# One decoder layer on one core: block sums of h on VectorE, the last denominators, merged heads in halves, order of loads

## The chip, the cores and the metric

The kernel runs on one core of one Trainium2 chip. The metric is the device time of one execution in microseconds (us); the figure given for a kernel is the median of its runs.

## What is computed

One inference step of a decoder layer for a prompt of 1024 tokens and 8 sample tokens (T = 1032 columns, model width 1024 = 8 blocks of 128). What matters here:

```python
h = rms_norm(x, g_pre)
q, k, v, c_b, c_c, c_h, g_a, g_c = split(h @ w_in)       # 4608 + 5 * 1024 columns
# three head groups with (window, dilation) (128,1), (512,4), (2048,16), 8 heads of 64 each;
# the groups of a head are merged by softmax over their log-denominators
a = merge(attention(q, k, v)) @ w_attn_o                 # 512 -> 1024
c = (c_b * causal_conv3(c_c * c_h)) @ w_conv_o
x = x + rms_norm((sigmoid(g_a) * a + sigmoid(g_c) * c) @ w_o)
x = x + rms_norm(square(relu(rms_norm(x) @ w_ff1)) @ w_ff2)
```

The sample tokens attend to caches of 128, 512 and 1024 rows, and all three caches go out again shifted by one row.

## The kernel before

Every float32 product is split: an operand is a rounded high part and a low part, and a product is three matrix products on TensorE (high by high, high by low, low by high). Weights come from HBM in tiles of 128x512 (SyncE's queue, L169), ScalarE casts the high part (L177) and VectorE or GpSimd subtracts to get the low part (L180). A `plan` lists the weight tiles in the order of their use; `tick`, called after each unit of matmuls, moves tiles through load, sum, cast and subtraction. Tile tracks what each instruction depends on and reorders instructions on each engine; those given to `keep_in_program_order` (`pe`, `pin`) keep the written order among themselves on their engine. A pool that opens where another was closed lies on the same memory, so the first writer of a new tile waits for the last reader of the old ones, a DMA too.

**Attention of the prompt.** A loop over 8 head slots h: scores, maximum, exponentials, products with v. `fill(h)` is a generator that gives the projections of the next head slot in units of 12 matmuls (128x344), run between the steps so that TensorE always has work. For h = 7 there is no next slot: `fill(7)` projects v and then four raw gates (`gate_raw`, L375), 30 units, of which 28 are used up before the loop's end. `den_out(h)` (L745) splits the sums of exponentials (`parts`), yields, reduces them over partitions by four matmuls (L752), copies the row (`den_row`, L753) and stores it in DRAM (`den_d`, L754, on GpSimd's queue); its first half normally runs in the next head slot. `num_d` holds the unnormalised heads in four pairs. `copy_piece(4)` issues four of 57 DMAs that copy caches to their outputs, on ScalarE's queue.

**Block products.** The remaining projections of h by pairs of weight blocks use Strassen's seven products (`strassen`, L1039) instead of eight. They need sums of blocks of h, T1 to T4 (`tsums`, L998): h cut into upper and lower four row blocks (`js`, `ks`) and left and right halves of columns (`t1`, `t2`), 516 columns each. `tsums(0)` and `tsums(2)` each make half of the rows, as operations on 128x1032 elements: T1 and T2 by five subtractions and additions on VectorE, T3 by one, T4 by two on GpSimd; ScalarE casts the high part of T2, T3 and T4 (L1005), VectorE the low part of T2 and T3, GpSimd that of T4 (L1006). They run beside two more raw gates (12 units). At the end T1 is written over the right half of h itself (L1035, L1036). Product p of a Strassen pair reads, in order: T2, h upper left, h upper right (that is T1), T3, h lower left, T4, h lower right. Each product has two parts of 12 matmuls (128x258); one part is called a beat here, 14 beats a pair. The results gather in three accumulators A, B, C of two banks each; after p = 1, 3, 4, 5 and 6 ScalarE and VectorE move them out (L1058 to L1068), and p = 3 goes on in B.

**Drive.** Fourteen pairs run under `drive` (L1099), which also carries out the attention of the sample tokens (`sample_steps`, 72 steps): in two beats of five it takes one step. The first steps transpose q, k and v of the samples (L821, L833), load the denominators, take their reciprocal (L809) and store it (`rden_d`); then come pipelines that load cache rows, multiply on GpSimd and sum on VectorE. The tiles of this stage (E, D1, the tiles of the samples) lie where the sums' pool was.

**Last three pairs and merged heads.** The three pairs left over (`gate_pairs`) run with `split_heads` (L1161) beside them, one step a beat, 37 steps in 42 beats: for each of four pairs of heads, load numerators (512 KB) and reciprocal denominators (2 x 256 KB, broadcast over partitions) on GpSimd's queue, six beats later multiply on VectorE (L1170), then cast and subtract each half (L1175, L1176) into `ah`, `al`. D0 and D1 receive the results and are stored from GpSimd's queue (L1118).

**Projections of attention and convolution.** For i in 8 blocks: `load_gate` (GpSimd's queue, L1207) and `load_cv` (ScalarE's queue, L1212), four buffers each; sigmoid of the gate (L1220), products with `wao`, gating of the result on VectorE (L1224), store of it (L1233), and the split of the convolution's result (L1229, L1230). Then follow the products with w_conv_o and w_o and the two of the MLP.

Of the kernel before, what the change touches and what calls it, by code (L numbers as in the profile page):

```python
# [10 lines left out]
F32 = mybir.dt.float32  # L11
# [7 lines left out]
P = 128  # L19
# [18 lines left out]
def tile_decoder_layer(  # L38
# [253 lines left out]
    def run(g, n=None):  # L292

        while n is None or n > 0:
            if next(g, run) is run:
                return
            n = n and n - 1
# [72 lines left out]
    def copy_piece(n=1):  # L370
        for _ in range(n):
            if pieces:
                tc.keep_in_program_order(nc.scalar.dma_start(*pieces.pop(0)))
# [9 lines left out]
    with ExitStack() as st:  # L383
# [11 lines left out]
        def classes(t):  # L395

            return t.rearrange("p (r j) -> p r j", r=4)
# [374 lines left out]
        for h in range(8):  # L772
            f = fill(h)
            run(dn, 1)
            for j, _ in enumerate(qk_scores()):
                if j in (2, 4, 6, 8):
                    run(f, 1)
                if j == 5:
                    run(dn)
            maximum()  # L780
            run(f, 3)
            max_keys()
            run(f, 2)
            subtract()
            long = h in (2, 4, 6, 7)
            run(f, 5 if long else 3)
            v_place(vts["v01"], 0, 0)
            v_place(vts["v01"], 1, 1)
            if h % 2 == 0:
                v_place_pair(vts["v2"])  # L790
            run(f, 2 if long else 3)
            for j, _ in enumerate(pv_out(h)):
                if long or j % 4 != 1:
                    run(f, 1)
            dn = den_out(h)
            run(f)
            copy_piece(4)
        run(dn)


    def sbank(shape, name):
# [190 lines left out]
    with tc.tile_pool(name="tsum", bufs=1) as ts:  # L992
        T1 = ts.tile([P, 4, HT], F32, name="T1")

        def f32(x):
            return x.bitcast(F32)

        def tsums(j):  # L998
            js, ks = slice(j, j + 2), slice(4 + j, 6 + j)

            def new(name, bufs=1):
                return ts.tile([P, 2, HT], F32, name=name, bufs=bufs)

            def parts(eng, n, t):
                nc.scalar.copy(TS[n][0][:, js], t)  # L1005
                eng.tensor_tensor(TS[n][1][:, js], t, f32(TS[n][0][:, js]), op=OP.subtract)  # L1006
            V, G, S = nc.vector.tensor_tensor, nc.gpsimd.tensor_tensor, OP.subtract
            b12, b22, T2 = new("b12", 2), new("b22", 2), new("T2", 2)
            V(b12, f32(hh[:, js, t2]), f32(hl[:, js, t2]), op=OP.add)
            V(b22, f32(hh[:, ks, t2]), f32(hl[:, ks, t2]), op=OP.add)  # L1010
            V(T1[:, js], b12, f32(hh[:, js, t1]), op=S)
            V(T1[:, js], T1[:, js], f32(hl[:, js, t1]), op=S)
            V(T2, b22, T1[:, js], op=S)
            yield
            parts(nc.vector, 2, T2)
            yield
            yield
            T3, T4 = new("T3"), new("T4")
            V(T3, b22, b12, op=S)
            parts(nc.vector, 3, T3)  # L1020
            G(T4, f32(hh[:, ks, t1]), T2, op=S)
            G(T4, T4, f32(hl[:, ks, t1]), op=OP.add)
            parts(nc.gpsimd, 4, T4)
            yield

        def plain():
            for i in (8, 9):
                yield from gate_raw(i, ts.tile([P, T], F32, name="gr", bufs=2))
        g = plain()
        for _ in zip(tsums(0), tsums(2)):  # L1030
            run(g, 2)
        run(g)
        for j in (0, 2):
            js = slice(j, j + 2)
            nc.scalar.copy(hh[:, js, t2], T1[:, js])  # L1035
            nc.vector.tensor_tensor(hl[:, js, t2], T1[:, js], f32(hh[:, js, t2]), op=OP.subtract)  # L1036
# [38 lines left out]
    with ExitStack() as st:  # L1075
# [23 lines left out]
        def drive(g):  # L1099
            for _ in g:  # L1100
                beat[0] += 1
                store(3)
                if beat[0] % 5 in (1, 3) or short[0]:
                    short[0] = next(steps, None)


# [49 lines left out]
    with tc.tile_pool(name="apool", bufs=1) as apool:  # L1156
# [3 lines left out]
        with tc.tile_pool(name="pre", bufs=1) as pre:  # L1160
            def split_heads():  # L1161
                for n in range(4):
                    ar, rd = (pre.tile([P, NQ], F32, name=nm) for nm in ("num", "rden"))
                    nc.gpsimd.dma_start(ar, num_d[:, n, :])
                    for a in range(2):
                        nc.gpsimd.dma_start(rd[64 * a:64 * a + 64, :],
                                            rden_d[2 * n + a:2 * n + a + 1, :].to_broadcast([64, NQ]))
                    for _ in range(6):
                        yield
                    nc.vector.tensor_tensor(ar, ar, rd, op=OP.mult)  # L1170
                    yield
                    for c in range(2):
                        src = ar.rearrange("p (r j) -> p j r", r=4)[:, P * c:P * c + P]
                        hi, lo = (t[:, n, 512 * c:512 * c + 512].rearrange("p (j r) -> p j r", r=4) for t in (ah, al))
                        nc.scalar.copy(hi, src)  # L1175
                        nc.vector.tensor_tensor(lo, src, hi.bitcast(F32), op=OP.subtract)  # L1176
                        yield
                nc.scalar.copy(ah[:, :, NQ:], asm)
                nc.vector.tensor_tensor(al[:, :, NQ:], asm, ah[:, :, NQ:].bitcast(F32), op=OP.subtract)
                yield  # L1180
            heads = split_heads()
            for pair in gate_pairs:
                D = [pre.tile([P, T], F32, name=f"D{a}") for a in range(2)]
                if pair is gate_pairs[-1]:
                    raw_spaces.pop()
                    nc.gpsimd.dma_start(gr0, g_d[8])
                for _ in strassen(pair, D, stores(D, [g_d[m - 60] for m in pair], None, False)):
                    run(heads, 1)
            run(heads)
            nc.scalar.activation(gr0, gr0, AF.Sigmoid)  # L1190
# [6 lines left out]
        with tc.tile_pool(name="cpool", bufs=1) as cpool:  # L1197
# [3 lines left out]
            with tc.tile_pool(name="sga", bufs=1) as sga:  # L1201
                cvs, grs = [], [gr0]

                def load_gate():
                    if len(grs) < KT:
                        grs.append(sga.tile([P, T], F32, name="gr", bufs=4))
                        nc.gpsimd.dma_start(grs[-1], g_d[7 + len(grs)])  # L1207

                def load_cv():
                    if len(cvs) < KT:  # L1210
                        cvs.append(sga.tile([P, T], F32, name="cv", bufs=4))
                        nc.scalar.dma_start(cvs[-1], cv_d[len(cvs) - 1])  # L1212
                for _ in range(2):
                    load_gate()
                    load_cv()
                for i in range(KT):
                    load_gate()
                    load_cv()
# [363 lines left out]
```

## Time and profile before

| what | value |
| --- | --- |
| median of 3 runs (lowest, highest) | 2033.48 us (2033.07, 2035.68) |
| the profiled execution: its time, its span | 2032.52 us, 2030.7 us |
| mean granted clock of TensorE | 0.983 of full speed |
| TensorE (PE) busy | 1955.0 us, 96% |
| VectorE (DVE) busy | 1243.6 us, 61% |
| ScalarE (ACT) busy | 735.3 us, 36% |
| GpSimd (POOL) busy | 602.6 us, 30% |

The span runs from the first to the last instruction; the execution's own time is 1.8 us more. TensorE is busy nearly all the time, so what is worth looking at is where it is not, and what ended each of its waits. In a row of the timeline, the bracket at the end names how long the engine was idle before it and what released it; where several things were waited for, the row names one.

### The profile page before, as it was taken

What the parts mean: (1) busy time and instruction counts of PE and PEld (TensorE: products, weight loads), DVE (VectorE), ACT (ScalarE), POOL (GpSimd) and SP (SyncE); (2) the same over time, 40 slices, a digit from 0 to 9 for tenths busy, and PEclk for the clock granted to TensorE, in tenths of its full rate; (3) what the DMA queues carried; (4) which work ended last, traced back from release to release, by engine and by line L of the source; (5) the groups of instructions that cost most, each with busy time, mean ns of one, the idle gap of its engine ahead of it and who ended that gap; (6) DMA issues with size and microseconds to landing.
All of it is one profiled execution on the core that took longest, in us unless ns stands there. A gap on an engine that the chain in (4) does not pass through costs nothing. (4 is left out here: it accounts for less than half of the span.)

```text
span 2030.7 us, 33252 instructions
## 1 busy us (share of the span) xinstructions
PE 1955.0 (96%) x13253; PEld 1932.2 (95%) x13253; DVE 1243.6 (61%) x2086; ACT 735.3 (36%) x1448; POOL 602.6 (30%) x487
## 2 busy tenths in 40 slices
PE   7999999999998899999999999999999999999996
PEld 6999999999998799999999999999999999999995
DVE  7688768777756787897554423735544444454545
ACT  4355435544442333333343333452222222222242
POOL 3233313332334674662412222211111111111113
PEclk8999999999999899999999999999999999999998
DMA  4221343144334363331665431322222322222102
GB/s 146 59 87 38 108 131 128 59 129 131 111 101 164 113 205 109 126 116 54 186 251 165 138 102 46 94 91 86 84 94 84 125 94 84 94 94 83 53 22 84
DMA packets 85995, 216.74 MB, mean 107 GB/s; under 512 B 12000, under 2 KB 22368, under 8 KB 84944
## 3 DMA queue, kind: packets, MB, share of 16 engines
q1 hardware_dynamic: 68736, 119.12, 18.2%
q10 hardware_dynamic: 8112, 68.78, 10.0%
q0 software_dynamic: 8992, 26.72, 4.4%
q8 instruction: 104, 1.70, 0.3%
q14 instruction: 51, 0.42, 0.1%
HBM read 184.17 MB, written 84.86 MB: 132 GB/s over the span
## 5 line engine op out<-in xcount | busy, mean ns | idle before, releaser
L180 POOL TENSOR_TENSOR wl<-wr,wh 128x512 fp32r<-128x512 f32 x152 | 201.9, 1329 | 804.4 <-ACT wh L177 707.6
L177 ACT CAST wh<-wr 128x512 fp32r<-128x512 f32 x320 | 195.3, 619 | 526.5 <-PE ps_mm L260 272.4
L257 PE MATMUL ps_mm<-hh,wh 128*128 128x344 f32 x1008 | 329.7, 327 | 2.5 <-ACT hh L346 1.9
L260 PE MATMUL ps_mm<-hl,wh 128*128 128x344 f32 x1008 | 324.2, 322 | 3.7 <-DVE hl L340 1.9
L261 PE MATMUL ps_mm<-hh,wl 128*128 128x344 f32 x1008 | 323.4, 321 | 0.0
L261 PE MATMUL ps_mm<-rh,wl 128*128 128x344 f32 x768 | 246.4, 321 | 0.0
L257 PE MATMUL ps_mm<-rh,wh 128*128 128x344 f32 x768 | 246.4, 321 | 0.0
L260 PE MATMUL ps_mm<-rl,wh 128*128 128x344 f32 x768 | 245.7, 320 | 0.0
L260 PE MATMUL ps_mm<-gl,wh 128*128 128x344 f32 x768 | 244.9, 319 | 0.8 <-DVE gl L1303 0.8
L257 PE MATMUL ps_mm<-gh,wh 128*128 128x344 f32 x768 | 245.5, 320 | 0.0
L261 PE MATMUL ps_mm<-gh,wl 128*128 128x344 f32 x768 | 244.7, 319 | 0.0
L1419 DVE TENSOR_TENSOR f<-ps_mm,f 128x344 f32<-128x344 f32 x336 | 170.4, 515 | 111.5 <-PE ps_mm L261 110.9
L180 DVE TENSOR_TENSOR wl<-wr,wh 128x512 fp32r<-128x512 f32 x168 | 139.7, 832 | 152.8 <-ACT wh L177 152.4
L260 PEld LDWEIGHTS ps_mm<-hl,wh 128*128 128x128 f32 x1008 | 190.8, 189 | 5.7 <-DVE hl L340 3.2
L257 PEld LDWEIGHTS ps_mm<-hh,wh 128*128 128x128 f32 x1008 | 191.2, 190 | 3.9 <-ACT hh L346 2.9
L261 PEld LDWEIGHTS ps_mm<-hh,wl 128*128 128x128 f32 x1008 | 190.7, 189 | 0.0
L260 PEld LDWEIGHTS ps_mm<-gl,wh 128*128 128x128 f32 x768 | 144.2, 188 | 1.2 <-DVE gl L1303 1.1
L260 PEld LDWEIGHTS ps_mm<-rl,wh 128*128 128x128 f32 x768 | 144.8, 189 | 0.0
L261 PEld LDWEIGHTS ps_mm<-rh,wl 128*128 128x128 f32 x768 | 144.8, 189 | 0.0
L257 PEld LDWEIGHTS ps_mm<-rh,wh 128*128 128x128 f32 x768 | 144.8, 189 | 0.0
L257 PEld LDWEIGHTS ps_mm<-gh,wh 128*128 128x128 f32 x768 | 144.3, 188 | 0.0
L261 PEld LDWEIGHTS ps_mm<-gh,wl 128*128 128x128 f32 x768 | 144.1, 188 | 0.0
(326 smaller groups left out, 4555.0 us busy)
## 6 DMA issues: line engine op xcount, KB each, us to landing
wr<-in_win_dram SPq DMA_DIRECT2D x152, 256.0 KB
wr<-in_wf_dram SPq DMA_DIRECT2D x128, 256.0 KB
out_okv_dram<-in_cache_dram ACTq DMA_DIRECT2D x16, 1020.0 KB
kt<-in_cache_dram SPq DMA_DIRECT2D x32, 256.0 KB
x_sb<-in_xT_dram SPq DMA_DIRECT2D x12, 344.0 KB
cv_d<-D SPq DMA_DIRECT2D x16, 258.0 KB
gr<-g_d POOLq DMA_DIRECT2D x8, 516.0 KB, 7.4
cv<-cv_d ACTq DMA_DIRECT2D x8, 516.0 KB
```

The source lines that it names most:

```text
L177: pin_(nc.scalar.copy(hi, raw))
L180: pin_(eng.tensor_tensor(lo, raw, hi.bitcast(F32), op=OP.subtract))
L257: ins = nc.tensor.matmul(ps, wh, rh, start=(first and i == 0), stop=False)
L260: nc.tensor.matmul(ps, wh, rl, start=False, stop=False)
L261: nc.tensor.matmul(ps, wl, rh, start=False, stop=(last and i == n - 1))
L1419: pin(nc.vector.tensor_tensor(d, ps, d, op=OP.add))
```

## The change

The change has five parts. (1) In the last head slot the two units of projection left over are no longer run before the denominators: the split of the sums of exponentials comes first, then one unit, then the reduction, its copy and its store, then the last unit; and four cache copies are no longer issued there (all 57 are still made, in the MLP). (2) T4 and its low part move from GpSimd to VectorE. (3) The sample's steps begin after the first pair of the drive (beat 16 instead of 1). (4) The merged heads go in halves of 512 columns: eight loads of 256 KB and twice eight of 128 KB, four beats between load and use, then multiply and split at once; 41 steps in 42 beats. D0 of the last pairs gets a second buffer. (5) One convolution result fewer is loaded ahead of the loop over i.

```diff
--- before.py
+++ after.py
@@ -793,9 +793,13 @@
                 if long or j % 4 != 1:
                     run(f, 1)
             dn = den_out(h)
-            run(f)
-            copy_piece(4)
+            if h < 7:
+                run(f)
+                copy_piece(4)
+        run(dn, 1)
+        run(f, 1)
         run(dn)
+        run(f)
 
 
     def sbank(shape, name):
@@ -1001,10 +1005,10 @@
             def new(name, bufs=1):
                 return ts.tile([P, 2, HT], F32, name=name, bufs=bufs)
 
-            def parts(eng, n, t):
+            def parts(n, t):
                 nc.scalar.copy(TS[n][0][:, js], t)
-                eng.tensor_tensor(TS[n][1][:, js], t, f32(TS[n][0][:, js]), op=OP.subtract)
-            V, G, S = nc.vector.tensor_tensor, nc.gpsimd.tensor_tensor, OP.subtract
+                nc.vector.tensor_tensor(TS[n][1][:, js], t, f32(TS[n][0][:, js]), op=OP.subtract)
+            V, S = nc.vector.tensor_tensor, OP.subtract
             b12, b22, T2 = new("b12", 2), new("b22", 2), new("T2", 2)
             V(b12, f32(hh[:, js, t2]), f32(hl[:, js, t2]), op=OP.add)
             V(b22, f32(hh[:, ks, t2]), f32(hl[:, ks, t2]), op=OP.add)
@@ -1012,15 +1016,15 @@
             V(T1[:, js], T1[:, js], f32(hl[:, js, t1]), op=S)
             V(T2, b22, T1[:, js], op=S)
             yield
-            parts(nc.vector, 2, T2)
+            parts(2, T2)
             yield
             yield
             T3, T4 = new("T3"), new("T4")
             V(T3, b22, b12, op=S)
-            parts(nc.vector, 3, T3)
-            G(T4, f32(hh[:, ks, t1]), T2, op=S)
-            G(T4, T4, f32(hl[:, ks, t1]), op=OP.add)
-            parts(nc.gpsimd, 4, T4)
+            parts(3, T3)
+            V(T4, f32(hh[:, ks, t1]), T2, op=S)
+            V(T4, T4, f32(hl[:, ks, t1]), op=OP.add)
+            parts(4, T4)
             yield
 
         def plain():
@@ -1100,7 +1104,7 @@
             for _ in g:
                 beat[0] += 1
                 store(3)
-                if beat[0] % 5 in (1, 3) or short[0]:
+                if beat[0] > 14 and beat[0] % 5 in (1, 3) or short[0]:
                     short[0] = next(steps, None)
 
 
@@ -1160,17 +1164,17 @@
         with tc.tile_pool(name="pre", bufs=1) as pre:
             def split_heads():
                 for n in range(4):
-                    ar, rd = (pre.tile([P, NQ], F32, name=nm) for nm in ("num", "rden"))
-                    nc.gpsimd.dma_start(ar, num_d[:, n, :])
-                    for a in range(2):
-                        nc.gpsimd.dma_start(rd[64 * a:64 * a + 64, :],
-                                            rden_d[2 * n + a:2 * n + a + 1, :].to_broadcast([64, NQ]))
-                    for _ in range(6):
-                        yield
-                    nc.vector.tensor_tensor(ar, ar, rd, op=OP.mult)
-                    yield
                     for c in range(2):
-                        src = ar.rearrange("p (r j) -> p j r", r=4)[:, P * c:P * c + P]
+                        ar, rd = (pre.tile([P, 512], F32, name=nm) for nm in ("num", "rden"))
+                        js = slice(P * c, P * c + P)
+                        nc.gpsimd.dma_start(classes(ar), classes(num_d[:, n, :])[:, :, js])
+                        for a in range(2):
+                            nc.gpsimd.dma_start(classes(rd[64 * a:64 * a + 64, :]),
+                                                classes(rden_d[2 * n + a:2 * n + a + 1, :])[:, :, js].to_broadcast([64, 4, P]))
+                        for _ in range(4):
+                            yield
+                        nc.vector.tensor_tensor(ar, ar, rd, op=OP.mult)
+                        src = ar.rearrange("p (r j) -> p j r", r=4)
                         hi, lo = (t[:, n, 512 * c:512 * c + 512].rearrange("p (j r) -> p j r", r=4) for t in (ah, al))
                         nc.scalar.copy(hi, src)
                         nc.vector.tensor_tensor(lo, src, hi.bitcast(F32), op=OP.subtract)
@@ -1180,7 +1184,7 @@
                 yield
             heads = split_heads()
             for pair in gate_pairs:
-                D = [pre.tile([P, T], F32, name=f"D{a}") for a in range(2)]
+                D = [pre.tile([P, T], F32, name=f"D{a}", bufs=2 - a) for a in range(2)]
                 if pair is gate_pairs[-1]:
                     raw_spaces.pop()
                     nc.gpsimd.dma_start(gr0, g_d[8])
@@ -1210,9 +1214,9 @@
                     if len(cvs) < KT:
                         cvs.append(sga.tile([P, T], F32, name="cv", bufs=4))
                         nc.scalar.dma_start(cvs[-1], cv_d[len(cvs) - 1])
-                for _ in range(2):
-                    load_gate()
-                    load_cv()
+                load_gate()
+                load_gate()
+                load_cv()
                 for i in range(KT):
                     load_gate()
                     load_cv()
```

## Rows read from the trace of the kernel before

**Rows 1.** The page, part 1: engine, busy us, share of the span, instructions

```profile
PE 1955.0 (96%) x13253; PEld 1932.2 (95%) x13253; DVE 1243.6 (61%) x2086; ACT 735.3 (36%) x1448; POOL 602.6 (30%) x487
```

**Rows 2.** Waits of TensorE, whole run: total us, times, longest

```profile
PE ps_b L1051 <- DVE D L1059: 7.0, 4, 2.9
...
PE ps_mm L257 <- DVE gr L1224: 4.3, 1, 4.3
```

**Rows 3.** Timeline of TensorE, 643 to 673: start us, duration us

```profile
648.18 0.39 PE L1051 MATMUL ps_b<-t2h,wh 128*128 128x258 f32 x1 [4.28 <-ACT wh L177]
...
657.60 0.28 PE L1056 MATMUL ps_a<-hh,wl 128*128 128x258 f32 x1
668.79 1.87 PE L821 MATMUL ps_tq<-ident,qks 128*8 128x128 f32 x8 [10.91 <-ACT kt L824]
...
672.82 0.29 PE L1051 MATMUL ps_c<-hh,wh 128*128 128x258 f32 x1
```

**Rows 4.** Stretches: length, busy PE, PEld, DVE, ACT, POOL, clock, DMA, GB/s

```profile
644.80:667.20 22.40, 8.08 (x44) 7.02 (x44) 22.18 (x12) 10.16 (x15) 17.50 (x8) 0.74 0.24 82
...
668.70:672.60 3.90, 3.81 (x19) 3.22 (x20) 1.92 (x6) 2.51 (x9) 2.47 (x6) 0.51 0.16 42
...
915.00:945.00 30.00, 30.00 (x249) 29.41 (x248) 22.74 (x37) 10.57 (x21) 10.89 (x8) 1.00 0.14 45
964.00:1024.00 60.00, 53.34 (x420) 51.94 (x419) 36.62 (x55) 23.67 (x39) 21.84 (x29) 0.97 0.59 172
1034.00:1080.00 46.00, 41.72 (x254) 41.19 (x253) 24.46 (x45) 20.55 (x32) 7.46 (x14) 0.96 0.82 292
```

**Rows 5.** Timeline of VectorE, 615 to 668

```profile
624.93 1.23 DVE L1009 TENSOR_TENSOR b<-hh,hl 128x1032 f32<-128x1032 f32 x1 [8.87 <-ACT den_row L753]
...
635.24 1.22 DVE L1012 TENSOR_TENSOR T<-T,hl 128x1032 f32<-128x1032 f32 x1
636.49 3.34 DVE L1013 TENSOR_TENSOR T<-b,T 128x1032 f32<-128x1032 f32 x1
644.84 3.73 DVE L1006 TENSOR_TENSOR t2l<-T,t2h 128x1032 fp32r<-128x1032 f32 x2 [5.01 <-ACT t2h L1005]
...
650.17 0.68 DVE L180 TENSOR_TENSOR wl<-wr,wh 128x512 fp32r<-128x512 f32 x1
...
663.99 3.17 DVE L1036 TENSOR_TENSOR hl<-T,hh 128x1032 fp32r<-128x1032 f32 x1
```

**Rows 6.** Timeline of GpSimd, 633 to 645

```profile
633.16 5.58 POOL L1021 TENSOR_TENSOR T<-hh,T 128x1032 f32<-128x1032 f32 x1 [12.84 <-ACT gr L378]
...
642.05 0.53 POOL L754 DMA_DIRECT2D den_d<-den_row  x1
644.00 1.26 POOL L133 TENSOR_TENSOR s<-wr 128x512 f32<-128x512 f32 x1 [1.42 <-PE ps_mm L261]
```

**Rows 7.** Timeline of ScalarE (ACTq: its queue), 620 to 645

```profile
620.85 0.33 ACTq L380 DMA_DIRECT2D g_d<-vT  x1
621.21 2.75 ACTq L373 DMA_DIRECT2D out_okv_dram<-in_cache_dram  x4
...
643.76 2.00 ACT L1005 CAST t2h<-T 128x1032 fp32r<-128x1032 f32 x2 [6.92 <-DMA den_d<-den_row]
```

**Rows 8.** Tile num, 960 to 1030: ns min/median/max, first and last start us

```profile
L1170 DVE TENSOR_TENSOR num<-num,rden x4: 1225/1226/1470, 978.5 to 1015.1; 128x1024 f32<-128x1024 f32 x4
```

**Rows 9.** DMA issues, 960 to 1080: count, KB each, median us to landing

```profile
g_d<-D POOLq DMA_DIRECT2D x12, 258.0 KB, 3.7
...
num<-num_d POOLq DMA_DIRECT2D x4, 512.0 KB, 5.2
rden<-rden_d POOLq DMA_DIRECT2D x8, 256.0 KB, 4.4
```

**Rows 10.** Timeline of ScalarE, 1034 to 1076

```profile
1034.21 1.31 ACTq L1212 DMA_DIRECT2D cv<-cv_d  x3
...
1071.22 1.06 ACT L1220 ACTIVATE gr<-gr 128x1032 f32<-128x1032 f32 x1 [4.41 <-DMA gr<-g_d]
```

## Prediction, made before the change was run

> **What bounds the kernel now.** The page's first part says that TensorE is busy for 96% of the span [rows 1], so a change can win only where TensorE waits or runs slowly. The view of its waits names three places that the change touches [rows 2, 3]. I then read the timeline of each engine around them.
>
> First, the start of the block products. TensorE has run out of projections at 643.9 (the row at 648.18 less its 4.28 of idle time), starts product p = 0, stops again, ends p = 1 at 657.9 and stands still until 668.79; p = 2 starts at 672.82 [rows 3]. That is 28.9 us for 48 matmuls and 16 transposes. Undisturbed, a matmul of this shape takes 30.00 / 249 = 0.1205 us [rows 4], so the 48 are worth 5.8 us; eight transposes took 1.87 us at a granted clock of 0.51, the 1.2 GHz level, after 10.9 us of standing still [rows 3, 4], so about 0.95 us at 2.4 GHz, 1.9 us for both sets. Loss here: 28.9 - 5.8 - 1.9 = 21.2 us.
>
> Two queues make it. GpSimd starts T4 at 633.16 and needs 5.58 us for one operation, and the store of the denominators, whose row was copied by about 625 [rows 5], stands behind T4 and is issued only at 642.05 [rows 6]. T2's cast waits for that store, since its tile lies where `den_row` was: 643.76 [rows 7], though T2's first half is there when T4, which reads it, starts. The first sum of weight tiles on GpSimd (644.00) and so p = 0 come after it [rows 6]. From then VectorE works without a break until 667.2, writing T1 over h as its last act [rows 4, 5]; p = 2 reads that, and E and D1 lie where T1 was.
>
> Second, the last three pairs: of 60 us TensorE is busy 53.3, and the mean clock is 0.97 [rows 4], so 6.7 + 1.8 = 8.5 us are lost. VectorE waits in its queue for merged heads that are not loaded, or does two long splits in a row, and an accumulator is not moved out in time.
>
> Third, the attention projection: 46.0 - 41.7 = 4.3 us idle, and 0.04 x 46 = 1.8 us by the clock, 6.1 together [rows 4], because ScalarE's sigmoid waits 4.41 us for a gate [rows 10].
>
> **The change part by part.**
>
> *Denominators.* The reduction moves one unit forward on TensorE. Its store is issued near 620, when GpSimd has little to do, not at 642, and T2's cast no longer waits. VectorE's first operation moves little: it writes where vT was, so it needs the store issued at 620.85, and starts 4.1 us later [rows 5, 7]. That store is now issued some 0.8 us later (four matmuls come before the last unit), but no four large copies follow it on the queue [rows 7]. I take 624.3 instead of 624.9; between 623.5 and 625.7 all is possible. The copies move into the MLP, where TensorE does not wait for ScalarE's queue; their four issues cost 2.75 us of a queue with room.
>
> *T4 on VectorE.* Per half two operations and a low part move, six in all; VectorE then has 24 of 128x1032 in this stage instead of 18. Alone, one follows the other in (635.24 - 624.93) / 9 = 1.146 us [rows 5]: 27.5 us. Five low parts of weights, 0.60 us each (0.68 for one, less the overlap seen between neighbours), lie before the last write of h: 3.0 us. What GpSimd still does costs VectorE time: between 644.8 and 667.2 VectorE was busy 22.2 us with 12 instructions, seven large and five small, worth 8.0 + 3.0 = 11.0 us alone, beside 17.5 us of GpSimd [rows 4]; so 0.64 us for each us of GpSimd. Four sums of weight tiles stay, 1.26 us alone [rows 6], up to twice that beside VectorE: 3.2 to 6.4 us, I take 4.5. Sum: 624.3 + 27.5 + 3.0 + 4.5 = 659.3. T2's low part is done near 640, so p = 0 can start at 643.9 and p = 1 ends at 649.7; then TensorE waits for the last write of h, 9.6 us, and restarts at the lower level, which cost 1.9 us after the last such stop [rows 4]. The loss is 11.5 instead of 21.2 us: **9.7 us won**, 15 if GpSimd's sums fall into VectorE's idle time before 624, 5 if VectorE has holes of its own between dependent operations.
>
> *Sample's steps later.* They shift by 15 beats. Counted through, the 72 steps end at beat 193 of 196 instead of 178, so none is left over. Fifteen beats later the second pipeline meets the ends of four convolution rows instead of three; one of those meetings cost 2.9 us and a stretch of lower clock [rows 2]. I take 0, with 4 us either way. The last SyncE loads of this pipeline now run until three beats before the gates' pairs; the weights for them are loaded ahead.
>
> *Halves.* Now VectorE starts a head every (1015.1 - 978.5) / 3 = 12.2 us [rows 8], of which 5.2 us is the landing of 512 KB [rows 9] and 7.0 us work and queues, since the tiles have one buffer. Half the columns: 3.5 us, 4.4 us for 256 KB as `rden` shows [rows 9], and 0.3 us because three issues do not halve: 8.2 us for a half. The program leaves it five beats, 7.2 us. Eight halves take 65.6 us where 41 beats take 59.3; about 2 us are covered, as an accumulator is needed again only two beats after it is full. Loss 4.3 instead of 8.5: **4 us won**. With 3.7 us for a load of this size, as the stores show [rows 9], 7.5 us; with 10 us a half, 10 us lost. The second buffer of D0 takes away a wait of VectorE for a store and is in this. The Trainium skill, "DMA: Bandwidth & Descriptors", section "Anatomy of one DMA", puts a load from this queue at about 2.0 us plus its bytes over 436 GB/s, which speaks against 24 loads in place of 12; its figure would be 2.6 us for a half, shorter than these rows have it, and by it nothing would be lost here and the sum would be 4 us better.
>
> *Order of loads.* One of three convolution results loaded at 1034.21 [rows 10] goes back by one block. At 292 GB/s [rows 4] its 516 KB are 1.8 us of the queues, and the late gate hangs on two links (a store that frees a buffer, then the load). I take **3 us won** of 6.1; the ends are all of it, and 2 lost if the results now come late, since their casts stand before the sigmoids in ScalarE's queue.
>
> **Sum.** 9.7 + 0 + 4 + 3 = 16.7 us off the profiled execution's 2032.52. That stands 1.0 below the median of 2033.48, so I put the new median at 2016.5.
>
> **Rivals.** *All stops go* (0.16): VectorE ends its chain by 654, both later stages lose nothing, and the one costly meeting in the drive is gone: 15 + 8.5 + 6.1 + 4 less some 2 = 32 us, 2002. For it: each wait in rows 2 has its own remedy here. Against: VectorE's 24 operations are a hard 27.5 us.
>
> *VectorE becomes the bound of the block products' start* (0.16): the six moved operations stand before the low parts of T2 and of the weights, p = 0 starts late as well, and the other stages keep their waits; 5 us won, 2028. For it: VectorE has no idle time from 644.8 to 667.2 already. This is also what comes if the store of the denominators stays late in spite of its new place.
>
> *Slower* (0.08): the halved loads set the pace of the last three pairs. It decides from 8p - 61.3 - 8.5 = 12.7 us, p = 10.3 us a half; at 11 us the stage loses 26.7 instead of 8.5 and the total is 2039. For it: three issues a half pass through GpSimd's queue between stores that wait for VectorE, and 5.2 against 4.4 us says that half the bytes do not land in half the time. Against: GpSimd is busy only 21.8 of 60 us there [rows 4].
>
> **How the numbers follow.** My forecast has 0.60. A measurement of this kernel can tell 0.2%, 4 us, from no change. Faster: the forecast, the better case, and a bit over half of the third: 0.85. Same: the rest of it, 0.07. Slower: 0.08. The range goes to 2005, short of the better case's middle, and up to 2029, over the third.
>
> **What would show it.** After: no wait of T2's cast for the store; VectorE without GpSimd's T4, ending its chain near 659; TensorE idle once, about 10 us, before p = 2; no `ps_tq` transposes in the first pair; starts of L1170 some 7 to 8 us apart; a shorter wait before L1224. Wrong would be: idle time before p = 0, a chain ending past 664, starts of L1170 10 us apart, or new waits in the last drive pairs.

## The result, and the profile after

The changed kernel takes **2023.38 us** (median of four runs, 2021.37 to 2027.68). Before takes 2034.58 us in four runs on the same chip (2033.07 to 2038.88). The ratio is 0.9943 with a 95% interval of 0.9931 to 0.9955: a gain of 0.6%, clear of noise, 11.2 us in the medians. The profiled execution of the changed kernel takes 2023.48 us, its span 2021.7 us, 9.0 us less than the span before. The prediction has the sign, but the sum behind it fails: one term has the wrong sign, one is too large, and 5 us come from a place that the prediction never looked at.

The page's first part after the change (compare [rows 1]) shows nothing of this. TensorE's busy time is the same to 0.7 us.

```profile
PE 1954.3 (97%) x13253; PEld 1933.4 (96%) x13253; DVE 1235.1 (61%) x2096; ACT 736.4 (36%) x1448; POOL 606.0 (30%) x493
```

TensorE's waits over the whole run do show it (total us, times, longest; compare [rows 2]):

```profile
PE ps_b L1055 <- DVE D L1063: 8.2, 3, 5.6
PE ps_c L1059 <- DVE hl L1040: 5.0, 1, 5.0
PE ps_b L1055 <- DVE D L1065: 4.0, 2, 3.8
...
PE ps_mm L257 <- DVE gr L1228: 3.0, 1, 3.0
PE ps_sm L900 <- issue: 2.6, 1, 2.6
PE ps_c L1055 <- DVE D L1072: 2.4, 2, 1.9
```

The 10.9 us before the transposes are gone, and one wait of 5.0 us for the last write of h (L1040) is what is left of them. The waits for accumulators (L1063, L1065, L1072) have grown, and a new wait of 2.6 us stands in the drive (L900, the sample's row maxima).

To see where time went, I took six moments from the timeline of TensorE in each kernel: the start of the last matmul of the raw gates, then the starts of the first matmuls of the third pair of block products, of the last three pairs, of the attention projection and of the convolution's projection, and the end of VectorE (of its closing drain, 0.05 us after its last operation). The stretches between them, in us:

| stretch | before | after | difference |
| --- | --- | --- | --- |
| attention, to the last raw gate | 643.59 | 643.11 | -0.48 |
| start: to the third pair | 66.73 | 56.05 | -10.68 |
| drive: to the last three pairs | 253.35 | 253.03 | -0.32 |
| last three pairs | 70.35 | 78.66 | +8.31 |
| attention projection | 51.68 | 51.57 | -0.11 |
| all products after it, to VectorE's last operation | 935.05 | 934.38 | -0.67 |
| end: to the end of the span | 9.97 | 4.90 | -5.07 |

So the start won about what was forecast and the last three pairs gave most of it back. Where the forecast had 4 us won, 8.3 us were lost. And half of what remains was won behind the last operation of any engine.

**The start.** VectorE's timeline (start us, duration us, line, operation; compare [rows 5]):

```profile
624.45 2.25 DVE L1013 TENSOR_TENSOR b<-hh,hl 128x1032 f32<-128x1032 f32 x1 [8.86 <-DMA g_d<-vT]
626.62 2.31 DVE L1014 TENSOR_TENSOR b<-hh,hl 128x1032 f32<-128x1032 f32 x1
628.86 1.22 DVE L1015 TENSOR_TENSOR T<-b,hh 128x1032 f32<-128x1032 f32 x1
...
653.00 2.36 DVE L1040 TENSOR_TENSOR hl<-T,hh 128x1032 fp32r<-128x1032 f32 x2
655.29 1.22 DVE L1010 TENSOR_TENSOR t4l<-T,t4h 128x1032 fp32r<-128x1032 f32 x1
```

GpSimd's timeline beside it (compare [rows 6]):

```profile
619.82 0.53 POOL L754 DMA_DIRECT2D den_d<-den_row  x1
...
625.57 2.27 POOL L133 TENSOR_TENSOR wr<-wr 128x512 f32<-128x512 f32 x1
636.48 21.77 POOL L133 TENSOR_TENSOR s<-wr,s 128x512 f32<-128x512 f32 x1 [8.63 <-DVE wl L180]
658.21 1.28 POOL L133 TENSOR_TENSOR s<-wr 128x512 f32<-128x512 f32 x1
```

The store of the denominators is issued at 619.82, the chain begins at 624.45, and the last write of h is done at 655.4. GpSimd's sum at 636.48 lasts 21.77 us where its neighbour takes 1.28: it ends when VectorE's run of operations ends, and none of these took longer than 1.22 us.

**The last three pairs.** Window from the first matmul of these pairs to the first of the attention projection (columns as in [rows 4]), first before, then after:

```profile
963.67:1034.02 70.35, 63.69 (x507) 62.29 (x506) 42.02 (x65) 26.44 (x44) 23.47 (x32) 0.98 0.56 166
```

```profile
952.18:1030.84 78.66, 65.36 (x506) 63.97 (x505) 40.76 (x69) 26.47 (x44) 33.63 (x44) 0.93 0.47 148
```

TensorE is idle for 78.66 - 65.36 = 13.3 us instead of 6.7, and the clock fell from 0.98 to 0.93, which lengthened its work by 1.7 us. What it waits for stands in VectorE's timeline after the change, around the longest of these waits:

```profile
1006.85 0.69 DVE L1176 TENSOR_TENSOR num<-num,rden 128x512 f32<-128x512 f32 x1 [6.39 <-DMA rden<-rden_d]
...
1014.30 0.69 DVE L1176 TENSOR_TENSOR num<-num,rden 128x512 f32<-128x512 f32 x1 [3.55 <-DMA num<-num_d]
1016.12 1.05 DVE L1180 TENSOR_TENSOR al<-num,ah 128x512 fp32r<-128x512 f32 x1 [1.13 <-ACT ah L1179]
1017.09 0.42 DVE L1063 TENSOR_TENSOR D<-ps_b,D 128x258 f32<-128x258 f32 x1
```

and in TensorE's:

```profile
1017.56 0.58 PE L1055 MATMUL ps_b<-t3h,wh 128*128 128x258 f32 x1 [5.64 <-DVE D L1063]
```

The multiplication waits at the head of VectorE's queue for a load that has not landed. The move of the accumulator (L1063) stands behind it and behind the split, and TensorE stands for 5.64 us. The tile's own view (ns min/median/max, first and last start) gives the pace, and the view of DMA issues the landings (compare [rows 8, 9]):

```profile
L1176 DVE TENSOR_TENSOR num<-num,rden x8: 691/692/693, 963.5 to 1021.2; 128x512 f32<-128x512 f32 x8
```

```profile
g_d<-D POOLq DMA_DIRECT2D x12, 258.0 KB, 4.3
...
num<-num_d POOLq DMA_DIRECT2D x8, 256.0 KB, 3.7
rden<-rden_d POOLq DMA_DIRECT2D x16, 128.0 KB, 3.4
```

(1021.2 - 963.5) / 7 = 8.24 us from half to half.

**The end.** SyncE closes the program. Its waits in the last stretch, before and after (total us, times, longest):

```profile
SPq L1565 <- PEq L1565: 5.7, 2, 5.2
SPq L1565 <- DMA out_yT_dram<-f: 2.8, 1, 2.8
```

```profile
SPq L1569 <- DMA out_yT_dram<-f: 2.8, 1, 2.8
SPq L1569 <- PEq L1569: 0.6, 2, 0.5
```

The view names TensorE's sequencer, but that had long been done. The last store has landed at 2023.95 before and at 2019.98 after. Before, the instruction that is still running then is GpSimd's closing drain; every engine has one ahead of the final barrier. It is among the sequencers' records, which the views leave out: before it takes 13.09 us, from 2016.85 to 2029.94; after 6.55 us, from 2012.89 to 2019.44, so that it ends ahead of the last store's landing.

### The profile page after: what moved, and what is told of

Same layout as the page of the kernel before. It is cut to its first block, busy times and chain, and to the rows that moved or that the text cites. A ratio compares the mean times of both kernels' runs of the same rounds, so it can differ in the third digit from the quotient of the medians.

```text
span 2021.7 us, 33269 instructions
## 1 busy us (share of the span) xinstructions
PE 1954.3 (97%) x13253; PEld 1933.4 (96%) x13253; DVE 1235.1 (61%) x2096; ACT 736.4 (36%) x1448; POOL 606.0 (30%) x493
## 3 DMA queue, kind: packets, MB, share of 16 engines
q10 hardware_dynamic: 8112, 68.78, 10.1%
```

## The experiments

Eleven kernels, in three groups, each compared with before on the same chip (before: medians of 2033.7, 2034.5 and 2033.9 us in the groups). The stretches of their traces, in us, as in the table above, tell more than the times, since the first stretch alone, in which only part 1 edits anything (its last units), lay between 643.1 and 648.0, and between 643.6 and 647.3 in the three traces without part 1. Each trace is of one execution:

| kernel | median | ratio, 95% interval | start | drive | last three pairs | att. proj. | end |
| --- | --- | --- | --- | --- | --- | --- | --- |
| whole heads | 2024.01 | 0.9949 (0.9936, 0.9962) | 54.54 | 255.63 | 70.51 | 52.05 | 9.96 |
| parts 1 and 2 | 2024.15 | 0.9948 (0.9937, 0.9960) | 56.55 | 253.13 | 70.35 | 52.49 | 9.96 |
| part 4 alone | 2038.12 | 1.0019 (1.0010, 1.0028) | 66.82 | 253.23 | 77.01 | 51.99 | 4.91 |
| part 3 undone | 2025.93 | 0.9962 (0.9949, 0.9976) | 57.10 | 252.36 | 78.87 | 52.28 | 4.90 |
| two buffers | 2019.91 | 0.9928 (0.9915, 0.9940) | 54.49 | 253.81 | 73.05 | 50.45 | 4.90 |
| more issues | 2018.25 | 0.9918 (0.9905, 0.9931) | 54.55 | 256.97 | 69.82 | 49.91 | 4.92 |
| early drain | 2018.49 | 0.9921 (0.9908, 0.9933) | 54.47 | 253.61 | 70.29 | 51.21 | 4.91 |
| part 1 alone | 2031.55 | 0.9987 (0.9978, 0.9995) | 66.75 | 254.25 | 70.65 | 52.40 | 9.96 |
| part 2 alone | 2027.19 | 0.9968 (0.9957, 0.9980) | 59.62 | 253.85 | 70.21 | 51.56 | 9.96 |
| num twice | 2016.95 | 0.9920 (0.9905, 0.9934) | 54.52 | 256.05 | 68.95 | 51.44 | 4.92 |
| part 5 undone | 2026.23 | 0.9960 (0.9946, 0.9974) | 54.51 | 254.35 | 78.91 | 51.97 | 4.92 |

**Whole heads** (part 4 undone, D0 with one buffer again):

```diff
-                    for c in range(2):
-                        ar, rd = (pre.tile([P, 512], F32, name=nm) for nm in ("num", "rden"))
...
+                    ar, rd = (pre.tile([P, NQ], F32, name=nm) for nm in ("num", "rden"))
+                    nc.gpsimd.dma_start(ar, num_d[:, n, :])
...
-                D = [pre.tile([P, T], F32, name=f"D{a}", bufs=2 - a) for a in range(2)]
+                D = [pre.tile([P, T], F32, name=f"D{a}") for a in range(2)]
```

> The changed kernel with its merged heads whole again and one buffer for D0 (part 4 undone). Theory A: the halves set the pace of the last three pairs (eight of them at 8.25 us, the first issued 5.6 us after the first of these pairs begins), and cost 8 us against whole heads; this kernel is then 7 to 8 us faster than the changed one, about 2016, and the way from the first matmul of these pairs to the first of the attention projection is back from 78.7 to about 70 us. Theory B: the sample's steps, which end 15 beats later, are what slows these pairs (their DMAs and VectorE work run into them); then it stays within 2 us of the changed kernel, 2023, and the way stays near 78.

Theory A is right about the stage: 70.51 us instead of 78.66. But the time stayed where it was, 2024.01. VectorE's last operation came 4.5 us earlier than in the changed kernel, and the span ended 0.5 us later: the end took 9.96 us again, as before the change. So halves lengthen one stage and shorten the end, and the two about cancel. Theory B is out: the sample's steps end late here too.

**Parts 1 and 2 alone**, **part 4 alone**, **part 3 undone**. The edits are those of the diff; part 3 undone is

```diff
-                if beat[0] > 14 and beat[0] % 5 in (1, 3) or short[0]:
+                if beat[0] % 5 in (1, 3) or short[0]:
```

> The kernel before with parts 1 and 2 alone (denominators earlier, sums on VectorE). Theory A: the whole gain of the change lies here and nothing gives it back: product p = 2 of the first pair starts about 11 us earlier, and the time is 10 to 12 us under before, 2022.5, the last three pairs as before at 70 us. Theory B: the gain needs the later steps of the sample, whose transposes stand in the first pair: p = 2 starts 11 us earlier at most on paper, and the time is only 4 to 7 us under before.

> The kernel before with part 4 alone (halves, second buffer of D0). Theory A: 7 to 8 us slower than before, 2041, starts of the multiplication of a half 8 us apart, the last three pairs at 78 instead of 70 us. Theory B: within 2 us of before.

> The changed kernel with the sample's steps from beat 1 again (part 3 undone). Theory A: the first pair has its transposes and their wait behind the stop at p = 2 again, 2 to 4 us, and the drive loses its wait of 2.6 us at the row maximum's transposes elsewhere: within 3 us of the changed kernel, and the last three pairs still take 78 us. Theory B: 7 us faster than the changed kernel, with the last three pairs back at 70 us.

Parts 1 and 2 take the start from 66.73 to 56.55 us, 10.2 us, and leave the last three pairs at 70.35; the median, 2024.15, is 9.6 us under that of before. Part 4 alone makes these pairs 6.7 us longer and the end 5.1 us shorter; its ratio of 1.0019 is a small loss, 4.4 us in the medians, where 7 to 8 us were expected; the expectation did not count the end. With part 3 undone the pairs still take 78.87 us: theory B fails a second time. Part 3 shortens the start by 2.6 us against this kernel (57.10 to 54.5 in six traces; the changed kernel's own has 56.05, for a reason given below) and lengthens the drive: 253.0 to 257.0 us in the seven traces that have it, 252.4 to 254.3 in the six that don't.

**Two buffers** for num and rden, one for D0:

```diff
-                        ar, rd = (pre.tile([P, 512], F32, name=nm) for nm in ("num", "rden"))
+                        ar, rd = (pre.tile([P, 512], F32, name=nm, bufs=2) for nm in ("num", "rden"))
...
-                D = [pre.tile([P, T], F32, name=f"D{a}", bufs=2 - a) for a in range(2)]
+                D = [pre.tile([P, T], F32, name=f"D{a}") for a in range(2)]
```

> The changed kernel with two buffers for num and rden and one for D0 (the other way round in the changed kernel). Theory A: the single buffer makes the pace of the halves, since a half's loads are issued only when the half before has been read, so that landing and work add up to 8.25 us; with two buffers the starts of the multiplications follow the program, five beats or about 7.2 us apart, the last three pairs take 70 us or less instead of 78.7, and the time is 2014 to 2017. Theory B: the number of issues in GpSimd's queue and the stores of D set it: 76 to 79 us, and 2022 to 2025.

The multiplications now start on average (1001.4 - 964.6) / 7 = 5.3 us apart:

```profile
L1176 DVE TENSOR_TENSOR num<-num,rden x8: 679/687/2940, 964.6 to 1001.4; 128x512 f32<-128x512 f32 x8
```

So the single buffer made the pace, as theory A says, and the halves even run ahead of the program's five beats. The pairs lose 5.6 us less than in the changed kernel, but not all: 73.05 us, between the two theories, as is the time of 2019.91. One wait of 6.4 us is left, behind a multiplication of 2.94 us, its cast and its subtraction.

**Num twice**, rden once, D0 twice:

```diff
-                        ar, rd = (pre.tile([P, 512], F32, name=nm) for nm in ("num", "rden"))
+                        ar = pre.tile([P, 512], F32, name="num", bufs=2)
+                        rd = pre.tile([P, 512], F32, name="rden")
```

> The changed kernel with two buffers for num, one for rden, two for D0. Theory A: what is left in the last three pairs with two buffers for both and one for D0 (73.0 us) comes from D0's single buffer; here 68 to 70 us, and the time is 3 to 4 us under that kernel's, 2016. Theory B: it comes from VectorE and ScalarE doing a half in one go ahead of the accumulators (a multiplication of 2.94 us beside GpSimd's sums of weights, then a cast, then a subtraction): 72 to 75 us again, and 2019 to 2021.

68.95 us and 2016.95. This kernel differs from the changed one in nothing but the second buffer of num, and the stage is 9.7 us shorter: that is the plainest test of the single buffer. It is also 1.6 us under whole heads. Of the two theories the numbers are A's, but that D0's single buffer cost the 4 us against the kernel with two buffers is not shown. There VectorE waited once for a store of D0, 2.5 us, and TensorE did not wait with it; TensorE's longest wait, 6.4 us, stood behind the multiplication of 2.94 us, as in theory B. Here the multiplication ahead of the longest wait takes 0.90 us, and a wait of 4.7 us behind a half stays:

```profile
PE ps_b L1055 <- DVE D L1063: 5.0, 2, 4.7
```

**More issues** and **early drain**, both with whole heads:

```diff
-                        nc.gpsimd.dma_start(m2, m2_d[i, :, s])
+                        if len(todo) < 12:
+                            nc.gpsimd.dma_start(m2[:64], m2_d[i, :64, s])
+                            nc.gpsimd.dma_start(m2[64:], m2_d[i, 64:, s])
+                        else:
+                            nc.gpsimd.dma_start(m2, m2_d[i, :, s])
```

```diff
                 run(done)
+                if end:
+                    pin(nc.gpsimd.drain())
                 if not end:
```

> The kernel with whole heads (the first experiment), in which twelve of the later loads of m2 are issued as two halves of 64 partitions: 133 DMA issues on GpSimd's queue, as in the changed kernel, with 8992 packets, as with whole heads. Theory A: the length of GpSimd's closing drain (13.09 us with whole heads, 6.55 us with halves) goes by the number of issues: 6.55 us here, and the time is 5 to 6 us under the first experiment's 2024.0, about 2018.5. Theory B: it goes by the packets or by something else in the halves: 13.09 us, and 2024.

> The kernel with whole heads (the first experiment) with one more drain of GpSimd, put behind its last sum of the second third of the columns, where it has nothing to do for 11.5 us. Theory A: a drain works off what GpSimd's DMAs have left behind: the early one takes 13.1 us beside TensorE's work, the closing one under 1 us, and the time is 4 to 6 us under the first experiment, about 2018.5 to 2019.5 (GpSimd's two last sums start 1.6 us later). Theory B: each drain takes its 13.1 us whatever ran before: the closing one is as long as ever, and the time is 2024 or a little more.

The drains, from the records of the sequencers:

```
kernel        drain: start, us    GpSimd's DMA issues, packets    last packet    end of span
before        2016.85, 13.09      121, 8992                       2023.95        2030.71
whole heads   2008.35, 13.09      121, 8992                       2015.43        2022.20
after         2012.89,  6.55      133, 9184                       2019.98        2021.69
more issues   2009.57,  4.19      133, 9376                       2016.67        2018.40
early drain   1993.3,  11.64      121, 8992
              2006.06,  3.18                                      2013.16        2014.87
```

The closing drain is 13.08 to 13.09 us long in all five kernels with whole heads and no other edit of GpSimd's DMAs or drains, and 6.55 to 6.56 us in all six with halves, so it goes with the kernel and not with chance. The early drain takes the cost over: it begins with the last sum of the second third, which takes 1.64 us, and lasts 10.0 us more. The closing one then lasts 3.18 us, until GpSimd's own two last sums are done:

```profile
1993.34 1.64 POOL L1467 TENSOR_TENSOR f<-f,x 128x688 f32<-128x688 f32 x1 [1.30 <-DVE f L1464]
2005.31 3.87 POOL L1467 TENSOR_TENSOR f<-f,x 128x688 f32<-128x688 f32 x2 [10.34 <-DVE f L1464]
```

That is theory A of this run: beyond those sums (3.1 us) 0.1 us is left of the closing drain. The end is 5.05 us shorter, the medians are 5.5 us apart (2024.01 and 2018.49; against before on the same chip, 9.7 and 16.0 us won). With more issues the end is as short, 4.92 us, but the drain is 4.19 us long, which neither theory had. The packets were 9376 and not the 8992 of the expectation, so issues and packets both differ from whole heads; 133 issues go with 6.55 us in one kernel and with 4.19 in another, so their number alone doesn't set it. What does is open, and what a drain works off cannot be seen in the traces. What is shown is that edits of GpSimd's DMAs change the length of its closing drain by up to 9 us, that the end takes 9.96 or 9.97 us where that drain takes 13.09, and 4.90 to 4.92 where it takes 6.55 or less, and that a drain placed earlier takes the cost off the end.

**Part 1 alone** and **part 2 alone**, the edits as in the diff.

> The kernel before with part 1 alone (denominators before the last projections). Theory A: the store of the denominators was what held T2's cast and the first product; p = 0 starts at 643 to 644, but p = 2 still waits for VectorE, which is slowed by GpSimd's T4: 3 to 5 us under before, 2029 to 2031. Theory B: the late store was the whole delay of VectorE's chain: 9 us under before, about 2024.5, as with both parts.

> The kernel before with part 2 alone (T4 on VectorE, the denominators where they were). Theory A: GpSimd's T4 was the whole delay; without it the store of the denominators is issued as soon as its row is copied, and VectorE runs its sums at 1.15 us each: from the end of the raw gates to the third pair 56 to 57 us, as with parts 1 and 2 together (56.5), instead of 66.7, and the time is that of both, about 2024. Theory B: the late store holds T2's cast here too, through the memory it lies in: 60 us or more, and 2028 or more.

In its trace, part 1 alone starts p = 0 right behind the gates, 4.4 us earlier than before, stops again in p = 0 for 4.6 us, and has won nothing by the third pair (66.75): neither theory. By the medians it wins 2.9 us (2034.47 to 2031.55, by the interval 1.0 to 4.5), close to theory A; the trace is of the slowest of its eleven executions, 2037.21, and no stage of it shows where 2.9 us would come from. The trace has T2's second cast directly behind T4's, which waits for GpSimd (ScalarE, then VectorE):

```profile
648.25 1.05 ACT L1009 CAST t4h<-T 128x1032 fp32r<-128x1032 f32 x1 [10.57 <-POOL T L1026]
649.54 1.05 ACT L1009 CAST t2h<-T 128x1032 fp32r<-128x1032 f32 x1
```

```profile
650.63 2.25 DVE L1010 TENSOR_TENSOR t2l<-T,t2h 128x1032 fp32r<-128x1032 f32 x1 [7.12 <-ACT t2h L1009]
```

There the wait for the store was replaced by one for T4. Part 2 alone wins 7.1 us of the 10.2 in the stage and 6.7 in the medians, between its theories: the store is still issued late and still takes long to land, the first sum of weights waits for it, and T2's first cast starts only after it (639.94).

```profile
628.45 0.53 POOL L754 DMA_DIRECT2D den_d<-den_row  x1 [5.08 <-ACT den_row L753]
638.54 7.91 POOL L133 TENSOR_TENSOR s<-wr 128x512 f32<-128x512 f32 x1 [9.56 <-DMA den_d<-den_row]
```

Together they win 10.2 us in the stage and 9.6 in the medians: T4 is the larger cause, the denominators give the remaining 3 us once T4 is out of the way. Whether they give them without it too is open: the traces say no (0, 7.1 and 10.2 us for the first, the second and both), the medians add up (2.9, 6.7 and 9.6). That the store needs some 10 us to land here, and about 3 where the four cache copies are no longer issued just before it, fits the copies being in its way; it was not tried by itself.

**Part 5 undone** (two results ahead of the loop):

```diff
-                load_gate()
-                load_gate()
-                load_cv()
+                for _ in range(2):
+                    load_gate()
+                    load_cv()
```

> The changed kernel with two convolution results loaded ahead of the loop again (part 5 undone). Theory A: part 5 is worth about 1 us, not 3: from the start of the attention projection to that of the convolution's projection 52 to 53 us instead of 51.6, the rest as in the changed kernel, 2024 to 2025. Theory B: it is worth the 3 us of the forecast and chance hid it: 54.5 us, 2026 to 2027.

51.97 us against 51.57: the stage is just under theory A's 52 to 53, and not B's 54.5; the time, 2026.23, is B's, with a spread of 7.2 us over its seven runs. Over the seven traces with the new order the stage takes 51.27 us on average (49.91 to 52.28), over the six with the old order 52.02 (51.56 to 52.49): 0.75 us won, with ranges that overlap. The longest wait for a gate (at the line of `use_a`, L1224 before) is 2.1 to 4.0 us in the seven and 3.9 to 4.3 in the six. The two shortest stages, 50.45 and 49.91, are those with waits of 2.1 and 2.2 us, and the only two in which the granted clock stays at the upper level throughout.

## Why the prediction was right in its sign and wrong in its sum

| step | forecast | measured | by |
| --- | --- | --- | --- |
| start (parts 1, 2) | 9.7 won | 10.2 won | parts 1 and 2 alone |
| later steps (part 3) | 0 | 0.1 won, within a spread of 3.4 | start and drive, nine traces |
| halves (part 4) | 4 won | 6.7 to 8.3 lost | the last three pairs, three comparisons |
| order of loads (part 5) | 3 won | about 0.75 won | thirteen traces |
| closing drain | not there | 5.1 won | the end |

Part 3 is read from the start and the drive together: 309.7 and 309.5 us in the two kernels that have parts 1 and 2 without it (56.55 + 253.13, 57.10 + 252.36), 309.5 us on average in the seven that have all three (308.1 to 311.5). With 8.3 us lost on the halves the sum is about 8, the profiled executions are 9.0 apart, and the medians 11.2. The last 2 to 3 us of that are not explained by a stage; the changed kernel's four runs alone spread over 6.3 us. That the total came out as near as it did is in part luck: the halves missed their forecast by 11 to 12 us, and 5.1 us at the end, which the forecast did not have, made up for part of that. (Its own sum, 2033.48 - 16.7, is 2016.8; it wrote 2016.5.)

**Denominators and T4: right, by two errors that cancelled.** The chain was to start at 624.3 and started at 624.45; it was to end at 659.3 and ended at 655.4. Of the 3.9 us, 2.4 are in the term of 4.5 us for GpSimd's sums of weights: two of VectorE's operations took 2.25 and 2.31 us beside them, 2.1 us more than alone, and the sum at 636.48 cost VectorE nothing. The rest was miscounted: one of the 24 operations, T4's second low part (655.29), came behind the last write of h, and four low parts of weights came before it, not five, 1.15 and 0.6 us. The price of 0.64 us for each us of GpSimd, taken from the stretch before, held where GpSimd's operations came one after another (2.1 us for 3.4 here), not for the one that lasted through VectorE's run. The Trainium skill, "SBUF — State Buffer", section "Who interferes with whom", says that VectorE instructions with two inputs in SBUF contend with GpSimd's reads, and that the order of issue decides who is blocked; the 21.77 us of that sum beside VectorE's undisturbed 1.22 us agree that the two contend; which of the two is blocked by what order, this trace does not settle. The second error is the clock. These windows hold the start: before, with parts 1 and 2 alone, and after (each row ends with the granted clock, the DMA engines' share and GB/s):

```profile
643.60:710.30 66.70, 49.48 (x374) 46.65 (x374) 52.25 (x68) 28.00 (x56) 49.17 (x39) 0.87 0.36 113
```

```profile
645.10:701.60 56.50, 46.66 (x374) 44.82 (x374) 41.59 (x70) 22.72 (x49) 44.08 (x32) 0.91 0.36 115
```

```profile
643.10:699.20 56.10, 48.96 (x376) 47.51 (x375) 40.31 (x67) 22.84 (x49) 34.65 (x26) 0.91 0.22 68
```

With parts 1 and 2 alone TensorE's idle time fell from 17.2 to 9.8 us, by 7.4, where the forecast had 15.2 - 9.6 = 5.6; its busy time fell by 2.8 us, where the forecast had the other 4.1 from the clock. Together that is the 10.2 us. In the changed kernel, where part 3 takes the transposes out of the first pair too, idle time fell by 10.1 us but busy time by 0.5 only. There the granted clock is at the lower level (1.2 GHz) from 652.7, towards the end of the stop of 5.0 us, for 6.8 us, and a second time from 662.95, right behind a wait of 1.8 us for an accumulator, for 3.4 us; in the rest of the window it is at 2.4 GHz. The six other kernels with all three parts do not have the second fall, and their start takes 54.5 us instead of 56.05. The prediction credited the two causes in one sum; which of them wins how much by itself it did not say.

**Halves: the step that failed.** "Eight halves take 65.6 us where 41 beats take 59.3; about 2 us are covered, as an accumulator is needed again only two beats after it is full. Loss 4.3 instead of 8.5: 4 us won." The pace was right, 8.24 us for the 8.2 of the forecast. What it costs was not. First, the pairs begin at 952.18 and the first multiplication at 963.5, of which 5.6 us pass before the first load is issued (957.8), as 5.7 us did before the change (963.67 to 969.36); the comparison of 65.6 with 59.3 let the halves start with the pairs. Second, the cover did not exist: with one buffer each multiplication waits in VectorE's queue until its load has landed, 27.1 us in all, and the moves of the accumulators wait with it. VectorE's waits in these pairs, after the change:

```profile
DVE num L1176 <- DMA rden<-rden_d: 15.0, 3, 6.4
DVE num L1176 <- DMA num<-num_d: 12.1, 5, 3.5
```

A half that is late is paid for at once. 5.6 + 65.9 - 59.3 = 12.2 us would have been near the 13.3 us of idle time; that is worked out afterwards, but the two runs with second buffers test the cause: 73.05 us, and 68.95 with the second buffer of num as the only difference. The rival named *Slower* had this mechanism, and put its threshold for a slower kernel at 10.3 us a half; below that it was still a loss. The rule of the Trainium skill that the prediction set against its rows ("DMA: Bandwidth & Descriptors", section "Anatomy of one DMA") gave an estimate of 2.6 us for a half, by which nothing would have been lost. The 256 KB of num landed in 3.7 us at the median, so the trace does not agree with it here.

**Order of loads: mis-sized.** Of "3 us won of 6.1" about 0.75 came. The gate came earlier, but TensorE still waits for it: 3.0 us instead of 4.3 [rows 2]. On average over the thirteen traces the longest such wait is 2.9 us with the new order and 4.2 with the old. What holds it for the rest, the store that frees a buffer or the load behind it, was not tried.

**The end: missing.** The sum was made against the span and took its last 10 us as given. The wait of 5.2 us of SyncE's queue for the barrier was in the profile of before; no step looked there, and no part of the change aims at it.

The rivals *All stops go* and *VectorE becomes the bound* did not come: p = 0 starts 0.15 us behind the gates, and both later stages kept their waits. The new wait in the drive, 2.6 us at L900, is one of the signs that the prediction said would speak against it; it stands in all seven traces with part 3 and in none without, and is part of what the drive gives back.

## What to carry to other kernels

When a load is split into smaller pieces to start earlier, keep a second buffer: with one, landing and work add up in every piece, and a queue that also moves accumulators out passes each late landing on to TensorE. Price a pace by its waits in the queue where it stands, lead-in included, not by the difference of two rates. And look behind the last operation: in this kernel a change to DMA issues in the middle of the program moved the end by 5 us, more than some of the stages that were tuned, and one drain of GpSimd in an idle stretch took that cost away.

## What was not expected of the hardware

GpSimd's closing drain takes 13.09 us with 121 DMA issues, the last of them some 840 us earlier, 6.55 and 4.19 us with two other sets of issues, and 3.18 us when another drain ran before it; 3.1 us of each are GpSimd's last sums. A GpSimd sum of 1.28 us took 21.77 us beside an unbroken run of VectorE operations, and 21.75 to 21.77 us in all eight other kernels with parts 1 and 2.
